# An attention layer's two key triangles folded into one block of 128, and GpSimd weight splits cut into pieces of 256 columns

## The chip, the cores and the metric

The kernel runs on one core of a Trainium2 chip. The metric is the device time of one execution in microseconds (us); of several runs the median is given. The engines are called as in the profile: PE (matmul) with PEld (its weight loads), DVE (vector), ACT (scalar), POOL (GpSimd) and SP, whose queue issues the DMA transfers.

## What is computed

A small decoder of two layers on an input of 2048 rows and 1024 columns in float32: first a gated retention layer, then a gated attention layer with a sliding window of 128 keys. The change lies in the second. Cut to what matters here:

```python
def band_bias_and_mask(rel_bias, nb):
    i = jnp.arange(BLOCK)[:, None]
    j = jnp.arange(2 * BLOCK)[None, :]
    dist = i + BLOCK - j
    ...
    in_window = (dist >= 0) & (dist < WINDOW)

def swa_layer(x, g_norm, w_in, g_q, sinks, w_out, k_band, v_band, bias, mask):
    proj = rmsnorm(x, g_norm) @ w_in
    q, gate = jnp.split(proj, [SWA_Q_WIDTH], axis=-1)
    q = rmsnorm(q.reshape(b, nb, BLOCK, SWA_KV_HEADS, SWA_GROUP, SWA_HEAD_DIM), g_q)
    scores = jnp.einsum('bnqkgd,bnjkd->bnkgqj', q, k_band).astype(jnp.float32)
    scores = scores * (SWA_HEAD_DIM ** -0.5) + bias[None, None]
    scores = jnp.where(mask[None, :, None, None], scores, -jnp.inf)
    m = jnp.maximum(jnp.max(scores, axis=-1, keepdims=True), sink)
    p = jnp.exp(scores - m)
    p = p / (jnp.sum(p, axis=-1, keepdims=True) + jnp.exp(sink - m))
    o = jnp.einsum('bnkgqj,bnjkd->bnqkgd', p.astype(v_band.dtype), v_band)
    o = o.reshape(b, s, SWA_Q_WIDTH) * jax.nn.silu(gate)
    return x + o @ w_out
```

BLOCK and WINDOW are both 128. A row block of 128 queries sees its own 128 keys and the 128 before. Query i may use key j of the block before when j > i, and key j of its own block when j <= i: for each j exactly one of the two. There are 16 query heads of 64 columns and 2 heads of keys and values, 8 query heads to each.

## The kernel before

Every projection is done in split precision. A weight tile of 128 partitions and 1024 columns (`wload`, L113) is loaded by SP, rounded by ACT into `whi` (L127), and the remainder is taken into `wlo` (L128 and L129): by DVE in the first layer and wherever a norm's scale has to be multiplied in first (L124), by POOL for all other weights of the second layer. `proj` (L132) then multiplies hi by hi, hi by lo and lo by hi: three matmuls where one would do in full precision, 24 of 512 columns to a tile.

The second layer is `phase_b` (L740). It works on four row groups of 512 rows (`g`) and, within each, on the two key heads (`kv`): eight units. Per unit there are these parts. `main` projects keys and values once per row group (`evac_kv`, L773: keys normalised, transposed and put into `kst`; values into `vst`) and then the queries (`evac_q`, transposed into `qst`, one half of them copied out of PSUM by DVE, L819, the other by ACT, L817). `gates` projects the gate. `attn` (L839) does the attention itself, `out_b` the output projection with the residual from memory; for the last unit `out_last` does it with the rows halved.

`attn` goes over four row blocks (`m`) and, in each, over two parities (`par`) with four heads `j` each; I call one parity of one row block a half block. Per half block: two matmuls per head give scores against up to 256 keys (L870). One DVE instruction (L873) adds the bias, negates, writes the result to `pt` and takes its least value over sink and row into `nm`. The bias is -1e30 where the window forbids a key. ACT takes the exponential with its row sum (L881). DVE adds the sink's term, takes the reciprocal and scales each head's row (L887). PE transposes each 128 by 128 piece (L891), four heads to a PSUM bank, one bank for each of the two key blocks `b`; ACT copies the first bank out (L897), DVE the second (L895). Once both parities are there, PE multiplies by the values (L907), block by block into one bank, and DVE and ACT apply the gate and split the result (L910 to L912). The very first row block has only its own keys, so `nb` is 1 there and 2 elsewhere.

Between row groups `stats` and `prep` (L183) make the next group's input: SP loads a tile, POOL multiplies it by the rows' norms (L189), ACT rounds it (L191) and DVE takes the remainder (L192), four times.

What order the work has: `drive` (L44) interleaves the parts by hand. `filler` (gates, the output projection of the unit before with the next group's prep in it, the next unit's `main`) and `attn` are generators, and `drive` takes them in turn by a ratio of 0.6, with `attn` issued at a higher priority (AHEAD). The order on each engine is then settled ahead of time by the framework's scheduler, from estimated durations; each engine works through its list in order. PSUM banks: two each for scores (`s`), for transposes and attention outputs (`f`), and four for projections.

## Time and profile before

| | us |
|---|---|
| median of 3 runs (2522.0 to 2522.67) | 2522.36 |
| the profiled execution | 2513.12 |
| its span, first to last instruction | 2511.3 |
| PE busy | 2446.6 |
| DVE busy | 1714.5 |
| ACT busy | 1128.1 |
| POOL busy | 477.2 |

The profiled execution is one run of its own, so its time differs a little from the median. Busy time of an engine is the union of its instructions; PE's includes modelled ends of pipelined matmuls. In a row of a group, "idle before" is the time in which the engine stood still just ahead of such an instruction, with what it waited for. In the chain of waits each piece is the work (or wait) that the end of the span depended on at that time. "Granted clock" is the share of full speed that PE was given: 1.00 is full.

### The profile page before, as it was taken

What the parts mean: (1) busy time and instruction counts of PE and PEld (TensorE: products, weight loads), DVE (VectorE), ACT (ScalarE), POOL (GpSimd) and SP (SyncE); (2) the same over time, 40 slices, a digit from 0 to 9 for tenths busy, and PEclk for the clock granted to TensorE, in tenths of its full rate; (3) what the DMA queues carried; (4) which work ended last, traced back from release to release, by engine and by line L of the source; (5) the groups of instructions that cost most, each with busy time, mean ns of one, the idle gap of its engine ahead of it and who ended that gap; (6) DMA issues with size and microseconds to landing.
All of it is one profiled execution on the core that took longest, in us unless ns stands there. A gap on an engine that the chain in (4) does not pass through costs nothing.

```text
span 2511.3 us, 32377 instructions
## 1 busy us (share of the span) xinstructions
PE 2446.6 (97%) x11816; PEld 1995.4 (79%) x11816; DVE 1714.5 (68%) x2953; ACT 1128.1 (45%) x2008; POOL 477.2 (19%) x393
## 2 busy tenths in 40 slices
PE   8999999999999999999999999989899999999998
PEld 6888787888888888888888888777677777777887
DVE  5546674786868657667666576677867677677766
ACT  4333233544436445435354354435544455445553
POOL 0000000021000020000010000042335444353360
PEclk9999999999999999999999999999899999999999
DMA  8434873586636455465364243374233342342432
GB/s 294 135 115 132 262 268 119 162 290 228 229 119 201 147 168 159 158 212 184 119 206 152 91 159 111 103 256 156 76 118 122 105 156 74 132 144 84 135 116 94
DMA packets 141035, 395.05 MB, mean 157 GB/s; under 512 B 16411, under 2 KB 28876, under 8 KB 140876
## 3 DMA queue, kind: packets, MB, share of 16 engines
q1 hardware_dynamic: 140876, 392.99, 47.3%
q8 instruction: 93, 1.52, 0.2%
q14 instruction: 66, 0.54, 0.1%
HBM read 321.60 MB, written 74.47 MB: 158 GB/s over the span
## 4 chain that ended last, share of the span: by engine, by line
PE 81%; DMA 8%; DVE 7%; ACT 2%; issue 1%; POOL 0%; SPq 0%; DVEq 0%; ACTq 0%
PE pp_ao L151 4%; PE pp_ao L149 4%; PE pp_ao L150 4%; PE o_t L907 2%; PE s_t L870 2%; PE pT_t L891 2%; PE pp_bo L149 1%; PE pp_bo L150 1%; PE pp_bo L151 1%; DMA res<-xmid 1%; PE ot_r L643 1%; PE dl_r L607 1%; PE o_r L615 1%; PE dl_r L608 1%; PE o_r L617 1%
## 5 line engine op out<-in xcount | busy, mean ns | idle before, releaser
L149 PE MATMUL pp_ao<-ohi_r,whi_ao 128*128 128x512 f32 x512 | 199.7, 394 | 4.9 <-DVE x_r L679 2.7
L150 PE MATMUL pp_ao<-olo_r,whi_ao 128*128 128x512 f32 x512 | 201.7, 394 | 0.0
L107 POOL TENSOR_SCALAR r_o_r<-sso_r,ep 128x1 f32<-128x1 f32 x48 | 28.6, 596 | 904.6 <-ACT jo_r L637 904.6
L881 ACT ACTIVATE P_t<-P_t,nm_t 128x256 f32<-128x256 f32 (+1 forms) x256 | 127.7, 499 | 157.3 <-DVE nm_t L873 156.7
L151 PE MATMUL pp_ao<-ohi_r,wlo_ao 128*128 128x512 f32 x512 | 196.7, 394 | 0.1
L873 DVE CUSTOM_DVE_ANT_0 P_t<-s_t,bias,nsnk 128x256 f32<-128x256 f32 (+1 forms) x256 | 116.5, 470 | 36.8 <-PE s_t L870 35.8
L127 ACT CAST whi_ao<-raw_ao 128x1024 fp32r<-128x1024 f32 x64 | 67.2, 1050 | 153.1 <-issue 47.5
L129 DVE TENSOR_TENSOR wlo_ao<-raw_ao,whi_ao 128x1024 fp32r<-128x1024 f32 x64 | 78.1, 1223 | 81.7 <-ACT whi_ao L127 80.3
L703 ACT CAST Shi_r<-S 128x512 fp32r<-128x512 f32 x120 | 69.9, 618 | 116.5 <-PE o_r L617 88.0
L149 PEld LDWEIGHTS pp_ao<-ohi_r,whi_ao 128*128 128x128 f32 x512 | 96.9, 189 | 26.0 <-DVE x_r L679 3.1
L151 PEld LDWEIGHTS pp_ao<-ohi_r,wlo_ao 128*128 128x128 f32 x512 | 97.1, 190 | 21.7 <-DVE wlo_ao L129 1.1
L150 PEld LDWEIGHTS pp_ao<-olo_r,whi_ao 128*128 128x128 f32 x512 | 97.4, 190 | 20.5 <-issue 0.2
L704 DVE TENSOR_TENSOR Slo_r<-S,Shi_r 128x512 fp32r<-128x512 f32 x120 | 85.4, 737 | 40.1 <-ACT Shi_r L703 39.9
L870 PE MATMUL s_t<-kst,qst_b 128*128 128x256 f32 (+1 forms) x512 | 103.3, 299 | 8.6 <-DVE nm_t L873 8.5
L870 PEld LDWEIGHTS s_t<-kst,qst_b 128*128 128x128 f32 x512 | 84.8, 193 | 30.8 <-DVE nm_t L873 11.5
L630 DVE SCALAR_TENSOR_TENSOR S<-S,dl_r 128x512 f32<-128x512 f32 x112 | 74.6, 682 | 41.4 <-PE dl_r L609 41.3
L887 DVE TENSOR_SCALAR P_t<-P_t,den_t 128x256 f32<-128x256 f32 (+1 forms) x256 | 95.0, 434 | 1.8
L679 DVE TENSOR_TENSOR x_r<-x_r,pp_ao 128x512 f32<-128x512 f32 x128 | 84.0, 683 | 14.1 <-PE pp_ao L151 14.0
L149 PE MATMUL pp_bo<-ohi_t,whi_bo 128*128 128x512 f32 x224 | 89.1, 406 | 1.3 <-DVE gate_b L834 1.1
L150 PE MATMUL pp_bo<-olo_t,whi_bo 128*128 128x512 f32 x224 | 89.0, 397 | 0.0
L129 POOL TENSOR_TENSOR wlo_bo<-raw_bo,whi_bo 128x1024 fp32r<-128x1024 f32 x28 | 70.5, 2523 | 93.9 <-ACT whi_bo L127 80.0
L151 PE MATMUL pp_bo<-ohi_t,wlo_bo 128*128 128x512 f32 x224 | 87.7, 396 | 0.0
(1037 smaller groups left out, 7464.1 us busy)
## 6 DMA issues: line engine op xcount, KB each, us to landing
raw_ao<-in_wo_a SPq DMA_DIRECT2D x64, 512.0 KB, 3.6
b<-in_w_vg SPq DMA_DIRECT2D x64, 256.0 KB, 5.1
res<-xmid SPq DMA_DIRECT2D x56, 256.0 KB, 3.0
raw_bo<-in_wo_b SPq DMA_DIRECT2D x28, 512.0 KB, 3.6
x_r<-in_x_t SPq DMA_DIRECT2D x16, 512.0 KB, 5.8
xin<-in_x SPq DMA_DIRECT2D x16, 512.0 KB, 3.5
xmid<-x_r SPq DMA_DIRECT2D x16, 512.0 KB, 4.3
xraw_b<-xmid SPq DMA_DIRECT2D x16, 512.0 KB, 3.6
```

Of the source, the lines that this page charges most:

```text
L129: eng.tensor_tensor(lo, raw, hi.bitcast(F32), op=ALU.subtract)
L149: nc.tensor.matmul(o, hi[:, kk, sl], xh, start=st, stop=False)
L150: nc.tensor.matmul(o, hi[:, kk, sl], xl, start=False, stop=False)
L151: nc.tensor.matmul(o, lo[:, kk, sl], xh, start=False, stop=sp)
L630: nc.vector.scalar_tensor_tensor(S32[:, d, :], S32[:, d, :], gamC[h], dl[d], op0=ALU.mult, op1=ALU.add)
L679: nc.vector.tensor_tensor(t, t, ps, op=ALU.add)
L703: nc.scalar.copy(hi, src[:, d, :])
L704: nc.vector.tensor_tensor(lo, src[:, d, :], hi.bitcast(F32), op=ALU.subtract)
L870: nc.tensor.matmul(o, qst[m][:, h, :], kst[:, kv * 2 + hl, kb + b0 : kb + 2, :], start=hl == 0, stop=hl == 1)
L873: nc.vector.tensor_tensor_reduce(out=pt[:, j, :w], in0=o, in1=bias[:, kv * GQ + h, b0 * P :], scale=-1.0, scalar=nsv[:, h : h + 1], op0=AL ...
L881: nc.scalar.activation(pt[:, j, :w], pt[:, j, :w], AF.Exp, scale=-1.0, bias=nm[:, c : c + 1], accum_out=den[:, c : c + 1])
L887: nc.vector.tensor_scalar_mul(pt[:, j, :w], pt[:, j, :w], den[:, c : c + 1])
```

## The change

In the attention, each pair of heads' 256 columns is folded: after the scores of two heads are reduced, DVE takes the minimum of the left and right 128 columns (the forbidden one of each pair is +1e30 after the negation). The exponential, its sum, the scaling (now one instruction for four heads) and the transposes work on 128 columns. Of the transposed bank ACT writes one copy as it is, and DVE a second one multiplied by a triangular mask, loaded once. The values are held twice: as they are, and as differences from the block before. The plain copy is multiplied by the values of the block before, the masked copy by the differences; their sum is the former result. The four exponentials of a half block are issued after all four score rows instead of each after its own.

Beside it: POOL takes a weight tile's remainder in four pieces of 256 columns instead of one instruction; the multiplication in `prep` goes from POOL to DVE; and two kinds of copies out of PSUM (the first half of the transposed queries, the transposed keys) go from DVE to ACT.

```diff
+PIECE = 256
...
-        eng = nc.gpsimd if psum["phase"] == "b" and kscale is None else nc.vector
-        eng.tensor_tensor(lo, raw, hi.bitcast(F32), op=ALU.subtract)
+        if psum["phase"] == "b" and kscale is None:
+
+            for k in range(kn):
+                for c in range(0, cols, PIECE):
+                    t = (slice(None), k, slice(c, c + PIECE))
+                    nc.gpsimd.tensor_tensor(lo[t], raw[t], hi[t].bitcast(F32), op=ALU.subtract)
+        else:
+            nc.vector.tensor_tensor(lo, raw, hi.bitcast(F32), op=ALU.subtract)
...
-            nc.gpsimd.tensor_tensor(raw, raw, rb.unsqueeze(1).to_broadcast([P, 2, T]), op=ALU.mult)
+            nc.vector.tensor_tensor(raw, raw, rb.unsqueeze(1).to_broadcast([P, 2, T]), op=ALU.mult)
...
+        mask = cst.tile([P, P], F32, name="mask_b")
+        nc.sync.dma_start(mask, mask_t)
...
-                vst = p2.tile([P, MT, KVH * HD], F32, tag="vst", name=f"vst_{n}")
+
+                vst = p2.tile([P, 2, MT, KVH * HD], F32, tag="vst", name=f"vst_{n}")
...
-                    nc.vector.tensor_copy(vst[:, m, :], kr[:, KVH * HD : 2 * KVH * HD])
+                    v = vst[:, 0, m, :]
+                    nc.vector.tensor_copy(v, kr[:, KVH * HD : 2 * KVH * HD])
+                    if g or m:
+                        before = (vst if m else st["kv", g - 1])[:, 0, (m - 1) % MT, :]
+                        nc.vector.tensor_tensor(vst[:, 1, m, :], v, before, op=ALU.subtract)
...
-                    nc.vector.tensor_copy(kst[:, :, kb + m + 1, :], tp.rearrange("p (a t) -> p a t", a=4))
+                    nc.scalar.copy(kst[:, :, kb + m + 1, :], tp.rearrange("p (a t) -> p a t", a=4))
...
-                    if half:
-                        nc.scalar.copy(dst, t3)
-                    else:
-                        nc.vector.tensor_copy(dst, t3)
+                    nc.scalar.copy(dst, t3)
...
+                        if j % 2 and nb == 2:
+
+                            pj = pt[:, j - 1 : j + 1, :]
+                            nc.vector.tensor_tensor(pj[:, :, :P], pj[:, :, :P], pj[:, :, P:], op=ALU.min)
                         if j == 3:
                             sn = snv.rearrange("p (j t) -> p t j", t=2)[:, par, :]
                             nc.vector.tensor_tensor(es[:, hs], sn, nm[:, hs], op=ALU.add)
                             nc.scalar.activation(es[:, hs], es[:, hs], AF.Exp)
-                        nc.scalar.activation(pt[:, j, :w], pt[:, j, :w], AF.Exp, scale=-1.0,
+                    for j in range(4):
+                        c = 4 * par + j
+                        nc.scalar.activation(pt[:, j, :P], pt[:, j, :P], AF.Exp, scale=-1.0,
                                              bias=nm[:, c : c + 1], accum_out=den[:, c : c + 1])
                     nc.vector.tensor_tensor(den[:, hs], den[:, hs], es[:, hs], op=ALU.add)
                     nc.vector.reciprocal(den[:, hs], den[:, hs])
+                    pw = pt[:, :, :P]
+                    nc.vector.tensor_tensor(pw, pw, den[:, hs].unsqueeze(2).to_broadcast([P, 4, P]), op=ALU.mult)
+                    tp = bank(f"pT_{n}_{m}_{par}", "f")
                     for j in range(4):
-                        c = 4 * par + j
-                        nc.vector.tensor_scalar_mul(pt[:, j, :w], pt[:, j, :w], den[:, c : c + 1])
+                        nc.tensor.transpose(tp[:, j * P : (j + 1) * P], pt[:, j, :P], ident)
+                    t = [p2.tile([P, 512], F32, tag=f"pT{par}", name=f"pTs_{n}_{m}_{b}_{par}") for b in range(nb)]
+                    nc.scalar.copy(t[0], tp)
+                    if nb == 2:
+
+                        a4 = lambda x: x.rearrange("p (a t) -> p a t", a=4)
+                        nc.vector.tensor_tensor(a4(t[1]), a4(tp), mask.unsqueeze(1).to_broadcast([P, 4, P]),
+                                                op=ALU.mult)
                     for b in range(nb):
-                        tp = bank(f"pT_{n}_{m}_{b}_{par}", "f")
-                        for j in range(4):
-                            nc.tensor.transpose(tp[:, j * P : (j + 1) * P],
-                                                pt[:, j, b * P : (b + 1) * P], ident)
...
-                    vv = (cur if blk >= 0 else prev)[:, blk % MT, kv * HD : (kv + 1) * HD]
+                    vv = (cur if blk >= 0 else prev)[:, 1 if b else 0, blk % MT, kv * HD : (kv + 1) * HD]
...
-                    nc.gpsimd.tensor_tensor(lo, raw, hi.bitcast(F32), op=ALU.subtract)
+                    for k in range(2):
+                        for c in range(0, T, PIECE):
+                            t = (slice(None), k, slice(c, c + PIECE))
+                            nc.gpsimd.tensor_tensor(lo[t], raw[t], hi[t].bitcast(F32), op=ALU.subtract)
```

More of the change, by code (lines that the diff above doesn't have):

```diff
@@ L138, in proj @@
             hi, lo = wload(src[kp], cols, f"{name}_{kp}",
-                           None if kscale is None else kscale[:, kp * kn : (kp + 1) * kn], (key, kp))
+                           None if kscale is None else kscale[:, kp * kn : (kp + 1) * kn],
+                           (key, kp))
             for kk in range(kn):
@@ L884, in attn @@
                     nc.vector.reciprocal(den[:, hs], den[:, hs])
+                    pw = pt[:, :, :P]
+                    nc.vector.tensor_tensor(pw, pw, den[:, hs].unsqueeze(2).to_broadcast([P, 4, P]), op=ALU.mult)
+                    tp = bank(f"pT_{n}_{m}_{par}", "f")
                     for j in range(4):
-                        c = 4 * par + j
-                        nc.vector.tensor_scalar_mul(pt[:, j, :w], pt[:, j, :w], den[:, c : c + 1])
-                    for b in range(nb):
-                        tp = bank(f"pT_{n}_{m}_{b}_{par}", "f")
-                        for j in range(4):
-                            nc.tensor.transpose(tp[:, j * P : (j + 1) * P],
-                                                pt[:, j, b * P : (b + 1) * P], ident)
-                        t = p2.tile([P, 512], F32, tag=f"pT{par}", name=f"pTs_{n}_{m}_{b}_{par}")
-                        if b:
-                            nc.vector.tensor_copy(t, tp)
-                        else:
-                            nc.scalar.copy(t, tp)
-                        pT[b, par] = t
+                        nc.tensor.transpose(tp[:, j * P : (j + 1) * P], pt[:, j, :P], ident)
[5 more added lines that the diff above has]
+                                                op=ALU.mult)
+                    for b in range(nb):
+                        pT[b, par] = t[b]
                     yield
```

## The prediction, made before the result

> **What bounds the kernel now.** I read the page's busy shares first, then the busy time by stretches of the second layer, then the chain of waits, then single groups. Busy shares:
>
> ```profile
> span 2511.3 us, 32377 instructions
> PE 2446.6 (97%) x11816; PEld 1995.4 (79%) x11816; DVE 1714.5 (68%) x2953; ACT 1128.1 (45%) x2008; POOL 477.2 (19%) x393
> ```
>
> The whole kernel is a queue of matmuls with everything else beside it. The change touches only the second layer, from about 1640 us on (and the hand-over into it), so I cut that into stretches; the columns are length, then busy time of PE, PEld, DVE, ACT and POOL, then the granted clock.
>
> ```profile
> core 0: us, PE busy (x) PEld busy (x) DVE busy (x) ACT busy (x) POOL busy (x), PEclk, DMA share, GB/s
> 1640.00:1726.00 86.00, 77.40 (x403) 65.69 (x402) 63.37 (x117) 37.92 (x67) 31.68 (x27) 0.94 0.68 239
> 1726.00:1781.00 55.00, 55.00 (x286) 44.16 (x286) 47.35 (x115) 30.47 (x74) 19.49 (x15) 1.00 0.36 122
> 1781.00:1804.00 23.00, 14.75 (x57) 9.25 (x55) 20.98 (x47) 11.59 (x29) 7.60 (x3) 0.63 0.35 115
> 1804.00:2010.00 206.00, 204.08 (x1070) 158.13 (x1070) 141.44 (x361) 97.27 (x240) 85.85 (x53) 1.00 0.32 106
> 2010.00:2030.00 20.00, 18.04 (x89) 14.64 (x88) 18.71 (x34) 13.20 (x28) 11.88 (x6) 0.91 0.45 152
> 2030.00:2215.00 185.00, 180.64 (x969) 142.44 (x968) 126.50 (x330) 91.48 (x224) 81.09 (x51) 1.00 0.32 108
> 2215.00:2265.00 50.00, 44.26 (x240) 35.08 (x239) 37.02 (x76) 23.91 (x55) 24.00 (x10) 1.00 0.55 186
> 2265.00:2456.00 191.00, 188.97 (x1021) 152.55 (x1019) 136.75 (x343) 102.21 (x245) 85.57 (x51) 1.00 0.34 112
> 2456.00:2512.00 56.00, 45.77 (x317) 37.64 (x315) 33.38 (x112) 16.43 (x53) 0.00 (x0) 0.95 0.25 85
> sum 872.00, PE 828.92 PEld 659.57 DVE 625.50 ACT 424.48 POOL 347.15; mean PE 92.10 PEld 73.29 DVE 69.50 ACT 47.16 POOL 38.57
> ```
>
> The three long stretches (582 us) have PE busy for 573.7 us, 98.6%: there the number of matmuls sets the time. The short stretches at 1781, 2010 and 2215 are where the next row group's input is prepared; DVE is nearly full there and PE stands still 8.3, 2.0 and 5.7 us, with the clock down to 0.63 in the first. DVE (72% of 872 us), ACT (49%) and POOL (40%) have room elsewhere.
>
> **The change part by part.** *Transposes.* The chain of waits gives what one projection matmul and what eight transposes hold of the path (start, length, engine, output, line, count):
>
> ```profile
> 2448.30 0.23 PE pp_bo L149
> ...
> 2451.85 0.87 PE pT_t L891 x8
> ```
>
> Group L891 (its row stands below) has 496 transposes. A full block has two key blocks times two head parities times four heads; folded, half of that: 60 banks of four go and 256 transposes stay. Four take half of 0.87, 0.435 us, and 60 x 0.435 = 26.1 us of PE. The product with the values stays at two matmuls per parity and block (plain values by all weights, differences by the masked ones), the scores stay, so nothing returns to PE. Where PE is 98.6% busy this is path. The four stretches where PE stands still (1781, 2010, 2215 and the tail from 2456) are 149 of the 872 us, 17%; a saving there may be lost in other waits. So 21.7 to 26.1, and I take 26.1.
>
> *DVE, ACT and POOL work.* First the groups that go, move or serve as prices (count | busy us, mean ns | idle before), then the least, median and greatest ns of one instruction of a line, last one exponential of 128 columns:
>
> ```profile
> L891 PE MATMUL pT_t<-ident_r,P_t 128*128 128x128 f32 x496 | 78.2, 281 | 1.0 <-ACT qst_b L817 0.4 <-ACT pTs_t L897 0.3 <-DVE P_t L887 0.2
> L887 DVE TENSOR_SCALAR P_t<-P_t,den_t 128x256 f32<-128x256 f32 x240 | 91.4, 444 | 1.7
> L895 DVE COPY pTs_t<-pT_t 128x512 f32<-128x512 f32 x60 | 41.3, 688 | 31.0 <-PE pT_t L891 31.0
> ...
> L819 DVE CAST qst_b<-qtp_b 128x512 fp32r<-128x512 f32 x32 | 21.9, 683 | 1.3 <-PE qtp_b L813 1.3
> L817 ACT CAST qst_b<-qtp_b 128x512 fp32r<-128x512 f32 x32 | 18.6, 582 | 5.5 <-PE qtp_b L813 5.4
> L189 POOL TENSOR_TENSOR xraw_b<-xraw_b,rb 128x1024 f32<-128x1024 f32 x16 | 43.0, 2692 | 32.1 <-DVE ssq_b L799 12.6 <-DMA xraw_b<-xmid 10.6 <-DVE rb L180 7.6
> ```
>
> ```profile
> L962 DVE TENSOR_TENSOR res_l<-res_l,pp_l x16: 412/422/423, 2476.8 to 2507.7; 128x256 f32<-128x256 f32 x16
> L805 DVE TENSOR_TENSOR qs_b<-qn_b,qs_b x32: 679/692/2868, 1702.7 to 2430.2; 128x512 fp32r<-128x512 f32 x32
> L192 DVE TENSOR_TENSOR xlo_b<-xraw_b,xhi_b x16: 1210/2109/3024, 1640.0 to 2234.3; 128x1024 fp32r<-128x1024 f32 x16
> L881 ACT ACTIVATE P_t<-P_t,nm_t x256: 387/509/544, 1713.1 to 2486.3; 128x256 f32<-128x256 f32 x120, 128x128 f32<-128x128 f32 x8
> L129 POOL TENSOR_TENSOR wlo_bo<-raw_bo,whi_bo x28: 2377/2406/3384, 1773.0 to 2444.6; 128x1024 fp32r<-128x1024 f32 x28
> L691 POOL TENSOR_TENSOR acc<-acc,sqx x28: 1259/1616/2138, 502.0 to 1662.0; 128x512 f32<-128x512 f32 x28
> ```
>
> ```profile
> 1804.13 0.40 ACT L881 ACTIVATE P_t<-P_t,nm_t 128x128 f32<-128x128 f32 x1 [3.48 <-DVE nm_t L873]
> ```
>
> DVE loses the scalings by 1/den (91.4 us), the second copy of a transposed bank (41.3) and the casts that go to ACT (32 at 21.9, and 16 of the keys at the same 0.68, 10.9): 165.5. It gets 120 minima of 2 x 128 columns at 0.42 (nearest row L962; as much as a 512-column row, 0.69, if the strided halves cost double), 50; 64 broadcast multiplications of 512 columns at 0.69 (L805), 44; 60 masked copies at 0.69, 41; 15 value differences at 0.42 at most (128 columns), 6; and the 16 multiplications of prep that POOL did, at the 1.21 of L192, 19. Sum 160 to 193: about even. ACT: 240 exponentials fall from 0.51 to 0.40 us, -26, and 48 casts come at 0.58, +28: even. POOL: 512 columns cost 1.26 and 1024 cost 2.38 at least, so 0.14 us an instruction and 0.56 per 256 columns; a piece takes 0.70 and a weight tile 2.8 instead of 2.4. With 86 tiles (28 and 4 of the output projections, 18 for each of three row groups) that is +34, against -43.0 for the prep work. All three have room beside PE in the long stretches, so I cost these totals at nothing; that cover is thin only in the first two prep stretches, where DVE is 91 and 94% busy; where it is gone, each us of DVE work is a us of PE.
>
> *The prep stretches.* The chain through the worst one, then POOL's own rows, then the same four scalings when POOL is quiet:
>
> ```profile
> 1776.04 2.29 DVE den_t L883
> 1778.56 5.44 DVE P_t L887 x4
> ...
> 1785.41 2.62 DVE xlo_b L192
> 1794.32 2.62 DVE xlo_b L192
> ```
>
> ```profile
> 1778.54 2.41 POOL L129 TENSOR_TENSOR wlo_bo<-raw_bo,whi_bo 128x1024 fp32r<-128x1024 f32 x1 [0.24 <-ACT whi_bo L127]
> 1780.90 2.42 POOL L189 TENSOR_TENSOR xraw_b<-xraw_b,rb 128x1024 f32<-128x1024 f32 x1
> ```
>
> ```profile
> 2470.85 1.06 DVE P_t L887 x4
> ```
>
> Four scalings take 5.44 us instead of 1.06 while two POOL instructions run back to back until 1783.3, and end 0.7 us after the second: DVE stands until POOL's instruction is over. The longest L192 lies 1.8 us over its least, the longest L805 2.2. In this stretch the holds on the chain are 4.4 (scalings), 1.9 or more (the sum L883 has four columns, and 256 need 0.42) and 2 x 1.4 (xlo): some 9 us. In pieces a hold is at most 0.70, and the second holder, L189, leaves POOL, for 4 x 1.21 us of DVE per prep. What PE loses in the stretch is 8.3 us of standing and (1 - 0.63) x 23 = 8.5 us of clock, 16.8; at 2010 it is 2.0 + 1.8; at 2215 5.7, of which most of the chain is the residual's round trip through memory, which stays. I take half of the first two and 1 us of the third: -11. Bounds: nothing, if the DVE work added fills what the holds free, and -22.
>
> The Trainium skill (SBUF — State Buffer, section Who interferes with whom) says that GpSimd and a DVE instruction that uses the second port or has two SBUF inputs exclude each other for a whole instruction, whichever came first. The 5.44 us agree. It also speaks against the change: the minima, the broadcast multiplication and the moved prep work have two SBUF inputs, so DVE may now hold POOL between pieces (third rival). The skill's TensorE: Matmul & The Clock Gate, section Part 1, says that an idle window of about 3.4 us halves the clock; if the standing goes, by that rule the 8.5 us go with it, which would make the sum some 4 us lower than mine.
>
> *The attention chain.* The scores' reduction stays, but a minimum follows each pair, and the four exponentials are issued after the second one. From the last score read to the first transpose, apart from a sum and a reciprocal that stay: before, the last exponential 0.51 and the scalings 1.06, 1.6 us; after, the minimum 0.42, four exponentials 4 x 0.40 and one multiplication 0.69, 2.7 us. That is 1.1 us longer per half block (one parity of one 128-row block, 64 in all). On DVE the third score read is queued behind the first minimum, and PE's next scores wait for that read to free their bank. PE's longest entry in the table of waits (us in total, times, longest):
>
> ```profile
> PE s_t L870 <- DVE nm_t L873: 8.5, 7, 3.2
> ```
>
> Seven waits for a score bank, and for P itself 0.2 us in all (end of the L891 row): the chain runs ahead of PE. I charge 0.42 for each of the seven, +3 (0 to +10, if 64 half blocks paid 0.16 each). The casts moved to ACT free their bank 0.6 us later per half, before scores that are a unit away: nothing, unless ACT is in a burst; it is 49% busy. The mask's load is one more transfer on SP's queue ahead of the first weights of the layer; its nearest row is
>
> ```profile
> 1670.09 0.48 SPq L738 DMA_DIRECT2D gk<-in_kng  x1
> ```
>
> so +0.5, in a stretch where PE waits for loads. Its prep multiplications pass from POOL to a DVE that is 74% busy there: 0, between -3 and +3.
>
> *Sum:* -26.1 - 11 + 3 + 0.5 = -33.6 us, against the profiled execution's 2513.1 us (span 2511.3). The median of the runs is 2522.4, 9.2 us above it; taking the difference over gives 2489 us.
>
> **The rivals.** *The prep stalls go entirely* (holds gone, clock up): -26 - 22 + 3 = -45, 2477. For it: the stall chain is made of holds. Against: 4.9 us of DVE work come into each of the three prep stretches. Chance 0.17.
>
> *The gain is swallowed.* The order of instructions is laid out anew from estimated durations; a few new waits of 2 to 4 us each at unit borders eat part of it: -21.7 + 10 + 3.5 = -8, 2514. For it: PE stands at such borders now, 4.4 us in the stretch from 2030. Chance 0.17, a quarter of it within 0.2% (5 us, about what a measurement of this kernel can tell from no change).
>
> *POOL falls behind.* If DVE takes the port after each piece for 0.69 us, a tile needs 4 x 1.39 = 5.6 us. PE takes 872 / 86 = 10.1 us per tile with the attention between, and POOL's other work (347 - 43 - 86 x 2.4 = 98 us) 1.1 of them. So from 9.0 us a tile on, tiles come late; at 0.5 us late each, 86 x 0.5 - 26 = +17, 2539, slower. For it: bursts of projection alone need a tile every 24 x 0.23 = 5.5 us. Against: even a 1.21 us hold after every piece gives 7.6. Chance 0.04.
>
> *The chain becomes the bound,* slower too: exposed fully, 64 x 1.1 = 70 - 26 = +44, 2566; it cancels the saving from 0.41 us per half block on. For it: it has two steps more. Against: PE hardly waits for P now, and a half block has 872 / 64 = 13.6 us of PE to hide 2.7 us in. Chance 0.03.
>
> **How the numbers follow.** Forecast 2489 with its own cases (2480 to 2500), 0.59. To 2470 for the full end of the stalls and of the saving, to 2512 for half of the swallowed case: that leaves out some 0.04 below and 0.15 above. Faster by over 0.2%: 0.59 + 0.17 + three quarters of 0.17 = 0.89; same 0.04; slower 0.07.
>
> **What would show it.** 256 transposes in group L891's place and 26 us less PE busy in the second layer; POOL pieces near 0.70 us; longest holds on DVE under 1 us; a granted clock of 1.00 around 1781 to 1804; PE's waits for score banks under 12 us. Wrong would be PE busy falling by 26 while the span does not: then the waits table names what came instead; or weight tiles from POOL among those that PE waits for.

## The result, and the profile after

The changed kernel takes 2534.39 us (median of 5 runs, 2531.89 to 2543.54), the kernel before 2522.36 (2519.37 to 2524.05). The ratio is 1.0054, 95% interval 1.0034 to 1.0074: slower by 12 us, where 33 us less were forecast. The profiled execution after took 2535.16 us. Its page begins:

```profile
span 2533.3 us, 32135 instructions
PE 2458.3 (97%) x11576; PEld 1977.5 (78%) x11576; DVE 1668.3 (66%) x2864; ACT 1126.1 (44%) x2056; POOL 501.4 (20%) x635
```

240 matmuls are gone, and PE is busy 11.7 us longer. The busy time by stretches shows the second layer, then the three stretches where PE now stands still (length, busy time of PE, PEld, DVE, ACT, POOL, granted clock):

```profile
1640.00:2534.00 894.00, 844.95 (x4223) 646.26 (x4221) 583.68 (x1443) 424.88 (x1058) 375.62 (x455) 0.97 0.37 124
```

```profile
1785.00:1808.00 23.00, 15.56 (x79) 10.77 (x78) 21.13 (x59) 16.45 (x49) 6.42 (x7) 0.85 0.39 134
2090.00:2110.00 20.00, 12.97 (x45) 6.72 (x44) 8.99 (x22) 9.18 (x23) 3.61 (x6) 0.76 0.09 27
2224.00:2240.00 16.00, 11.59 (x50) 8.58 (x47) 14.45 (x20) 9.66 (x16) 8.65 (x8) 0.79 0.31 102
```

The first stretch is the old prep stall: the clock falls less deep (0.85 for 0.63), but PE stands 7.4 us there, where it stood 8.3. The second is new: no engine is full there, so it is a chain that holds PE, not a load. The groups of the change, in the second layer (count | busy us, mean ns | idle before):

```profile
L925 PE MATMUL o_t<-pTs_t,vst_b 128*64 128x512 f32 x248 | 98.9, 633 | 6.9 <-DVE pTs_t L913 4.8 <-ACT pTs_t L909 2.0
L134 POOL TENSOR_TENSOR wlo_bo<-raw_bo,whi_bo 128x256 fp32r<-128x256 f32 x112 | 93.3, 866 | 87.7 <-ACT whi_bo L128 87.7
L892 DVE TENSOR_TENSOR P_t<-P_t 128x256 f32<-128x256 f32 x120 | 65.6, 558 | 1.3
L904 DVE TENSOR_TENSOR P_t<-P_t,den_t 128x512 f32<-128x512 f32 x64 | 46.7, 730 | 1.5
L907 PE MATMUL pT_t<-ident_r,P_t 128*128 128x128 f32 x256 | 45.0, 289 | 9.9 <-DVE P_t L904 9.6 <-ACT pTs_t L909 0.3
L913 DVE TENSOR_TENSOR pTs_t<-pT_t,mask_b 128x512 f32<-128x512 f32 x60 | 41.1, 685 | 27.1 <-ACT pTs_t L909 27.0
```

The transposes have 256 instructions and 33.2 us less busy time than the 78.2 before. But the products with the values (L925) have as many records, of the same shape, and take 98.9 us. Before, their row was:

```profile
L907 PE MATMUL o_t<-pTs_t,vst_b 128*64 128x512 f32 x248 | 68.4, 618 | 2.2 <-ACT pTs_t L897 2.2
```

The mean of one record hardly moved (618 to 633 ns); the busy time, which counts overlapping records once, rose by 30.5. So what changed is how far they overlap. PE's timeline shows it. One product (one head parity, one key block) is two records. Before, the four products of a row block:

```profile
1857.66 1.94 PE L907 MATMUL o_t<-pTs_t,vst_b 128*64 128x512 f32 x8
```

After, the four products of a row block:

```profile
1767.43 1.07 PE L925 MATMUL o_t<-pTs_t,vst_b 128*64 128x512 f32 x2
1768.43 0.50 PE L157 MATMUL pp_b1g<-xhi_b,whi_b1g 128*128 128x512 f32 x1
...
1772.64 1.08 PE L925 MATMUL o_t<-pTs_t,vst_b 128*64 128x512 f32 x4
1773.65 0.62 PE L882 MATMUL s_t<-kst,qst_b 128*128 128x256 f32 x3
1774.20 1.07 PE L925 MATMUL o_t<-pTs_t,vst_b 128*64 128x512 f32 x2
```

The weights are 64 columns wide (128\*64); the first parity writes partitions 0 to 63 of the output's bank, the second 64 to 127. Two products of different parity (x4) take 1.08 us, and one alone (x2) takes 1.07: in a pair the second starts 7 ns after the first and costs nothing. Before, four products filled two slots of about 1 us. Now the first one is issued alone, then a pair, then the last one alone: three slots. Counted in the trace, the products stand before in 25 unbroken runs of 8 records, 5 of 6, 1 of 4 and 7 of 2; after in 2 of 8, 9 of 6, 20 of 4 and 49 of 2. Two products to a slot where they can pair, that is 68 slots before and 91 after. From the first record of each run to the next other matmul, they hold PE 67.3 us before and 99.6 after.

To see where all the time went, I cut the second layer, from its first matmul (1654.2 us before, 1661.0 after) to the end, by the time from each matmul's start to the next one's; idle time then falls to the matmul that it follows. The layer starts 6.8 us later after the change; over all kernels here that start lies between 1652.6 and 1661.0, and at 1660.2 in the kernel before with only its products in another order, so I don't put it down to the change. "Half clock" is the time at which the granted clock is 0.5. "Lost" is PE's idle time and half of the time at half clock; "in prep" is the part of it in the three stretches in which the next row group is prepared, each from the first gate projection of a row group's second unit to the next group's first key projection. "Held" is the sum, over DVE's instructions, of the time beyond the shortest of the same line and shape. All in us, from one profiled execution of each kernel:

| kernel | layer 2 | PE idle | half clock | lost | in prep | products | transposes of P | scores | transposes of q, k | projections | held |
|---|---|---|---|---|---|---|---|---|---|---|---|
| before | 857.2 | 38.5 | 34.5 | 55.8 | 22.5 | 67.3 | 54.5 | 74.7 | 34.4 | 622.4 | 124 |
| after | 872.3 | 44.3 | 47.0 | 67.7 | 23.4 | 99.6 | 32.4 | 88.4 | 41.4 | 606.3 | 72 |
| pieces and moves | 846.0 | 28.8 | 33.7 | 45.6 | 19.2 | 67.6 | 53.3 | 78.8 | 31.9 | 610.4 | 67 |
| pieces alone | 848.8 | 32.6 | 29.9 | 47.6 | 14.0 | 69.4 | 54.7 | 77.1 | 33.3 | 610.6 | 71 |
| after, paired | 837.4 | 42.5 | 42.1 | 63.6 | 22.9 | 63.7 | 29.3 | 86.9 | 40.3 | 612.9 | 64 |
| fold alone | 887.5 | 55.2 | 58.0 | 84.2 | 29.1 | 99.2 | 33.5 | 99.0 | 33.4 | 618.5 | 133 |
| fold alone, paired | 865.4 | 60.4 | 73.5 | 97.2 | 37.4 | 67.5 | 28.6 | 102.4 | 34.9 | 628.2 | 139 |

Before to after: transposes -22.1, projections -16.1, products +32.3, scores +13.7, transposes of queries and keys +7.0; sum +14.8 of the +15.1. The first term is the gain that was forecast for the transposes. The second is for the most part standing that has changed its place: PE stands 12.5 us less behind projections and 18.3 us more behind the other matmuls, and what it loses in the prep stretches is as before (22.5 and 23.4). The third is not in the prediction at all; without the standing and the loss at half clock behind the products it is +26.0 (64.0 to 90.0).

### The profile page after: what moved, and what is told of

It is laid out like the page before. It is cut to its first block, busy times and chain, and to the rows that moved or that the text cites. A ratio compares the mean times of both kernels' runs of the same rounds, so it can differ in the third digit from the quotient of the medians.

```text
span 2533.3 us, 32135 instructions
## 1 busy us (share of the span) xinstructions
PE 2458.3 (97%) x11576; PEld 1977.5 (78%) x11576; DVE 1668.3 (66%) x2864; ACT 1126.1 (44%) x2056; POOL 501.4 (20%) x635
## 4 chain that ended last, share of the span: by engine, by line
PE 80%; DMA 8%; DVE 7%; ACT 2%; issue 1%; POOL 1%; SPq 0%; DVEq 0%; ACTq 0%; POOLq 0%
PE pp_ao L159 4%; PE pp_ao L157 4%; PE pp_ao L158 4%; PE o_t L925 3%; PE s_t L882 2%; PE pp_bo L158 2%; PE pp_bo L159 2%; PE pp_bo L157 2%; DMA b<-in_w_vg 1%; PE pT_t L907 1%; PE ot_r L651 1%; PE dl_r L615 1%; PE dl_r L616 1%; PE o_r L623 1%; PE o_r L625 1%
## 5 line engine op out<-in xcount | busy, mean ns | idle before, releaser
L899 ACT ACTIVATE P_t<-P_t,nm_t 128x128 f32<-128x128 f32 x256 | 100.8, 394 | 118.0 <-DVE P_t L892 113.3
L134 POOL TENSOR_TENSOR wlo_bo<-raw_bo,whi_bo 128x256 fp32r<-128x256 f32 x112 | 93.3, 866 | 87.7 <-ACT whi_bo L128 87.7
L925 PE MATMUL o_t<-pTs_t,vst_b 128*64 128x512 f32 x248 | 98.9, 633 | 6.9 <-DVE pTs_t L913 4.8
L638 DVE SCALAR_TENSOR_TENSOR S<-S,dl_r 128x512 f32<-128x512 f32 x112 | 74.5, 681 | 41.4 <-PE dl_r L617 41.3
```

Source lines behind the costliest of these rows:

```text
L134: nc.gpsimd.tensor_tensor(lo[t], raw[t], hi[t].bitcast(F32), op=ALU.subtract)
L638: nc.vector.scalar_tensor_tensor(S32[:, d, :], S32[:, d, :], gamC[h], dl[d], op0=ALU.mult, op1=ALU.add)
L899: nc.scalar.activation(pt[:, j, :P], pt[:, j, :P], AF.Exp, scale=-1.0, bias=nm[:, c : c + 1], accum_out=den[:, c : c + 1])
L925: nc.tensor.matmul(op[par * HD : (par + 1) * HD, :], vv, pT[b, par], start=b == 0, stop=b == nb - 1)
```

## The experiments

**Theory A**: the products lost their partners, and these slots took the gain back. The rivals: the loss comes from the longer attention chain, from the PSUM banks, or from the other parts of the change.

**Pairs restored.** The changed kernel, with one dependency more.

```diff
-                    nc.scalar.copy(t[0], tp)
+                    cp = [nc.scalar.copy(t[0], tp)]
...
-                        nc.tensor.matmul(op[par * HD : (par + 1) * HD, :], vv, pT[b, par],
-                                         start=b == 0, stop=b == nb - 1)
+                        mm = nc.tensor.matmul(op[par * HD : (par + 1) * HD, :], vv, pT[b, par],
+                                              start=b == 0, stop=b == nb - 1)
+                        if par == 0:
+                            tc.add_manual_dep(mm.ins, cp[b].ins.name, mybir.DependencyInfo(
+                                mybir.DependencyClass.Sync, mybir.DependencyReason.DATA), reason="pair")
```

Here `cp` holds the second parity's copies when the products are written, so the first parity's product waits for its partner's data.

> The changed kernel, with one thing added: the first parity's product of a key block waits for the second parity's copy of the same block, so that the two products of a block stand next to each other in PE's order (62 slots of one or two products instead of 91; before the change 68). Theory A, lost pairs: two neighbouring products that fill different halves of the array run at once (1.01 us for the two, as for one alone), so 29 slots fewer are 29 us less: about 2505 us, 0.7% under the kernel before, and the group of products falls from 98.9 us busy to about 63. Rival B, the longer attention chain: the time went into waits for P and its copies; pairing makes products wait longer, so 2530 to 2545. Rival C, POOL's pieces or the moved work: pairing does not touch them, so no more than 5 us less than the changed kernel's 2534.

Measured: 2500.67 us, ratio to the kernel before 0.9929 (0.9912 to 0.9945). Against the changed kernel's 1.0054 that is 1.25%, some 31 us, for one added wait. PE's timeline has the four products of the same row block in two pairs, and the group's busy time is 66.0 us:

```profile
1772.13 1.08 PE L925 MATMUL o_t<-pTs_t,vst_b 128*64 128x512 f32 x4
1773.14 0.50 PE L882 MATMUL s_t<-kst,qst_b 128*128 128x256 f32 x2
1773.48 0.40 PE L159 MATMUL pp_b1g<-xhi_b,wlo_b1g 128*128 128x512 f32 x1
1773.81 1.08 PE L925 MATMUL o_t<-pTs_t,vst_b 128*64 128x512 f32 x4
```

```profile
L925 PE MATMUL o_t<-pTs_t,vst_b 128*64 128x512 f32 x248 | 66.0, 624 | 3.3 <-ACT pTs_t L909 2.7 <-DVE pTs_t L913 0.6
```

By the table the products give back 35.9 us (99.6 to 63.7), the whole layer 34.9 (872.3 to 837.4). Theory A stands, and this version beats both kernels.

**The kernel before, its products in another order.** The two loops around the products exchanged:

```diff
-                for b in range(nb):
-                    blk = m - 1 + b0 + b
-                    vv = (cur if blk >= 0 else prev)[:, blk % MT, kv * HD : (kv + 1) * HD]
-                    for par in range(2):
+                for par in range(2):
+                    for b in range(nb):
+                        blk = m - 1 + b0 + b
+                        vv = (cur if blk >= 0 else prev)[:, blk % MT, kv * HD : (kv + 1) * HD]
```

> The kernel before, with the two loops around the products exchanged (parity outside, key block inside), which leaves every instruction and only changes PE's order: 93 slots instead of 68. Theory A: 25 slots more at 1.0 us, so about 2547 us, 1.0% slower than before, and the group of products near 93 us busy. Rivals B and C: nothing but the order of four neighbouring products changes, so within 3 us of before.

Measured: 2524.82 us, ratio 1.0019 (1.0009 to 1.0029), 4.6 us and not 25: a miss. The trace shows why, and it sharpens the theory. The four products still stand next to each other, and although the program's order is now parity 0, 0, 1, 1, they take the same 1.94 us:

```profile
1769.35 1.94 PE L907 MATMUL o_t<-pTs_t,vst_b 128*64 128x512 f32 x8
```

Their records start in pairs 13 ns apart, where it was 7; which product a record belongs to the trace does not say. So this order inside an unbroken run does not matter; in these traces a product is alone only when matmuls of another kind stand between it and its partner. The products held PE 67.6 us, as before.

**One PSUM bank.** The changed kernel, where the output's bank now can't be had before the second parity's transposes are copied:

```diff
-PSUM_BUFS = {"rr": 4, "s": 2, "f": 2}
+PSUM_BUFS = {"rr": 4, "s": 2, "f": 1}
```

> The changed kernel, with one PSUM bank instead of two for transposes and attention outputs. It tests why the order changed. Theory A says: in the changed kernel a half block needs one transposed bank instead of two, so the output's bank is free before the second parity is transposed and the first product is issued alone; with one bank it can't be. The order built from it has 62 slots, as in the run with the pairs kept: about 2505 us if the missing bank costs nothing, up to 2525 if transposes have to wait for copies. Rival B (the chain from scores to products sets the time): one bank lengthens that chain, so slower than the changed kernel, 2540 or more.

Measured: 2566.99 us, ratio 1.0188 (1.0172 to 1.0203). All products stand in pairs in the program's order, which agrees with the reading of the code that the freed bank is what lets the first product go early: before, four transposed banks pass through the two banks ahead of the output's, in the changed kernel two. But a single bank makes PE wait for each copy:

```profile
PE o_t L925 <- DVE pTs_t L913: 21.5, 10, 3.8
PE pT_t L907 <- DVE pTs_t L913: 16.3, 9, 4.4
```

PE's idle time in the layer goes to 83.9 us. As a cure it is worse than the loss.

**Without the fold.** The kernel before with the pieces on POOL, the prep multiplication on DVE and the copies on ACT, by the lines of the change's own diff:

```diff
+                    nc.gpsimd.tensor_tensor(lo[t], raw[t], hi[t].bitcast(F32), op=ALU.subtract)
...
+            nc.vector.tensor_tensor(raw, raw, rb.unsqueeze(1).to_broadcast([P, 2, T]), op=ALU.mult)
...
+                    nc.scalar.copy(kst[:, :, kb + m + 1, :], tp.rearrange("p (a t) -> p a t", a=4))
...
+                    nc.scalar.copy(dst, t3)
```

> The kernel before, with all of the change but the fold: POOL in pieces of 256 columns, prep's multiplication on DVE, the two kinds of casts on ACT. 70 slots of products, against 68 before. Theory A: no pairs are lost, so what is left is shorter holds of DVE against 36 us more of POOL: between 2510 and 2525, the prediction's own estimate being 11 us less than before. Rival C: these parts make the change slow, so 2532 or more.

Measured: 2510.9 us, ratio 0.9957 (0.9942 to 0.9973): 9 us faster. So the rest of the change is worth 9 to 11 us without the fold, and the fold as written costs what is left, 24 us. Only 3.3 us of the gain lie in the prep stretches (22.5 to 19.2).

**The fold alone**: the changed kernel without the pieces and the moves.

```diff
-                    nc.gpsimd.tensor_tensor(lo[t], raw[t], hi[t].bitcast(F32), op=ALU.subtract)
+        eng.tensor_tensor(lo, raw, hi.bitcast(F32), op=ALU.subtract)
...
-            nc.vector.tensor_tensor(raw, raw, rb.unsqueeze(1).to_broadcast([P, 2, T]), op=ALU.mult)
+            nc.gpsimd.tensor_tensor(raw, raw, rb.unsqueeze(1).to_broadcast([P, 2, T]), op=ALU.mult)
...
-                    nc.scalar.copy(dst, t3)
+                    if half:
+                        nc.scalar.copy(dst, t3)
+                    else:
+                        nc.vector.tensor_copy(dst, t3)
```

> The kernel before with the fold alone: GpSimd's subtractions whole, the multiplication of the residual stream on GpSimd, and the copies of transposed queries and keys on VectorE as before. The order that the scheduler writes for TensorE has 34 pairs of products with the values and 56 single ones, 90 slots, where the kernel before has 68. Theory A (a product that is cut off from its partner of the other parity takes about 1.0 us of its own, and in the changed kernel these slots take back what the 240 missing transposes give): the fold alone costs what the changed kernel costs over the run without the fold (ratios 1.0054 and 0.9957), 24 us, so about 2545, and in any case not under 2525. Theory B (the fold gains its 26 us, and the moved copies and pieces lose it): 2500 or less.

Measured: 2547.86 us, ratio 1.0115 (1.0101 to 1.013), 30 us slower than before. Theory A's 2545 holds; theory B, that the fold gains and the rest loses, is refuted.

**The fold alone, pairs restored**: both edits together.

> The fold alone, with the product of the first parity made to wait for the copy of the second parity, so that TensorE's order has 62 pairs and no single product. Theory A: 28 slots of 1.0 us less than the fold alone with single products, so 25 to 35 us faster than that kernel; against the kernel before it is worth what the paired run gained over the run without the fold (0.9929 against 0.9957), 7 us, so about 2513. If pairing only helps where ScalarE and VectorE carry the moved work, the two kernels with the fold alone lie within 8 us of each other.

Measured: 2524.8 us, ratio 1.0028 (1.0016 to 1.0041). The pairs give 22 us, a little less than the 25 to 35 expected, but the kernel is 7 us slower than before, not 7 faster. The parts don't add up: PE idles 60.4 us, against 42.5 with the whole change. Its waits, and DVE's minima:

```profile
PE pT_t L904 <- DVE P_t L901: 13.5, 6, 5.6
PE s_t L879 <- DVE nm_t L882: 12.7, 11, 2.9
```

```profile
L889 DVE TENSOR_TENSOR P_t<-P_t 128x256 f32<-128x256 f32 x120 | 82.7, 695 | 1.2
```

A minimum takes 0.70 us in the mean, with a median of 0.42 and a greatest of 2.62: DVE is held 139 us in all where the paired whole change has 64. With the paired fold the rest of the change is worth about 25 us (1.0028 to 0.9929), without it 9 to 11; the last runs ask which part.

**Exponentials earlier.** The paired kernel, with the exponentials of two heads right after the minimum of these two:

```diff
-                    for j in range(4):
-                        c = 4 * par + j
+                        if j % 2:
+                            for i in (j - 1, j):
+                                c = 4 * par + i
...
```

> The changed kernel with paired products, and the exponentials of two heads issued right after the minimum of these two heads, in place of after all four. In the paired run TensorE is busy 17.6 us less than in the run without the fold between 1640 us and the end, but idle 14 us more. Chain theory (this idle time is the half block's longer chain from scores to transposes, of which the late exponentials are one piece of about 1 us on each half block): 3 to 10 us faster than the paired run's 2500.7, so 2491 to 2498. Rival (ScalarE takes the exponentials in the same places anyway, because the scheduler fills it with other work, and the idle time comes from VectorE's two added steps, which stay): within 3 us of the paired run, 2498 to 2504.

Measured: 2503.13 us, ratio 0.9942 (0.993 to 0.9954), where the paired kernel has 0.9929 (0.9912 to 0.9945): no gain. The late exponentials are not what makes the chain long.

**Both parities in one half.** The kernel before, with an edit that lets all products write the first 64 partitions and leaves out the other half of the output:

```diff
-                        nc.tensor.matmul(op[par * HD : (par + 1) * HD, :], vv, pT[b, par],
-                                         start=b == 0, stop=b == nb - 1)
+                        nc.tensor.matmul(op[:HD, :], vv, pT[b, par],
+                                         start=b + par == 0, stop=b + par == nb)
...
-                nc.vector.tensor_tensor(og, og, op.rearrange("p (a t) -> p a t", a=4), op=ALU.mult)
+                nc.vector.tensor_tensor(og[:HD], og[:HD], op[:HD].rearrange("p (a t) -> p a t", a=4), op=ALU.mult)
```

> The kernel before, but all products with the values of a row block write and sum into the first 64 partitions of the output's bank, so that none lies beside a product of the other parity; the second 64 partitions of the gate are not multiplied, so the output is not the attention's. Number of instructions and their shapes are as before, neighbours in the order stay neighbours. Theory A (two neighbouring products take the time of one because they fill different column halves of the array): 124 slots of about 0.95 us where there were 68, so 50 to 58 us more busy time of TensorE, and 45 to 58 us slower than before, 2565 to 2580. Rival (neighbours overlap because nothing stands between them, whichever half they fill, as the exchanged loops might suggest, which cost only 4.6 us): the products take 67 us as before, and the kernel is within 6 us of the kernel before.

Measured: 2572.12 us, ratio 1.0208 (1.0191 to 1.0225): 54 us slower. The same eight records, side by side as before, take 3.65 us instead of 1.94:

```profile
1766.96 3.65 PE L907 MATMUL o_t<-pTs_t,vst_b 128*64 128x512 f32 x8
```

```profile
L907 PE MATMUL o_t<-pTs_t,vst_b 128*64 128x512 f32 x248 | 120.2, 623 | 2.1 <-ACT pTs_t L897 2.1
```

The mean record is again 623 ns and tells nothing; the union, 120.2 us, does. The products hold PE 119.0 us instead of 67.3, and these 51.7 us come out as 54 us of time: a slot of a product is on the path at its full price.

**Which part the fold needs.** Four runs: the kernel before with POOL's pieces alone (the first hunk of the diff of "Without the fold"); and the paired kernel less one part at a time, by the hunks of the diff of "The fold alone": with whole POOL tiles (the first), with the prep multiplication back on POOL (the second), and with the copies of queries and keys back on DVE (the third, and the same for `kst`).

> The kernel before with GpSimd's subtractions in pieces of 256 columns, and nothing else. The run without the fold gained 9.4 us with the pieces and the moved work together, and VectorE's time over the shortest duration of each of its instructions, which is where GpSimd holds it, fell from 130 to 69 us there. If the pieces did this (VectorE is held for at most one piece of 0.74 us, not for 2.4): 4 to 10 us faster than before, with VectorE's time over the minimum at 60 to 85 us. If the moved work did it (65 us less busy time of VectorE), the pieces alone are within 3 us of the kernel before.

> The changed kernel with paired products, but GpSimd's subtractions whole, 2.4 us each. Theory: the fold's new steps on VectorE have two inputs and are held by a long GpSimd instruction (in the run of the fold alone with paired products VectorE spent 144 us over the shortest durations, in the paired run of the whole change 67), and their ends stand in the chain from scores to transposes, so TensorE waits: 6 to 20 us slower than the paired run's 2500.7, 2507 to 2520. Rival (the moved copies made the difference between these two runs): within 4 us of the paired run.

> The changed kernel with paired products and pieces, but the multiplication of the residual stream (2.4 us each, whole) stays on GpSimd. VectorE has about 16 instructions of 1.2 us less, and is held by the long instruction in the stretches where the next group is prepared. If these holds are what stalls the stretches at 1790, 2010 and 2215 us, as the prediction had it: 3 to 8 us slower than the paired run, 2504 to 2509. If VectorE's load decides: 0 to 6 us faster, 2495 to 2501.

> The changed kernel with paired products and pieces, but the copies of the transposed keys and of half of the transposed queries stay on VectorE: about 48 copies of 0.6 to 0.7 us, some 30 us more busy time there and as much less on ScalarE. If VectorE's load makes the waits of the fold alone (60 us idle on TensorE where the paired run has 42): 8 to 18 us slower than the paired run, 2509 to 2519. If the long GpSimd instructions make them: within 4 us of the paired run's 2500.7.

Measured ratios to the kernel before: pieces alone 0.9953 (0.9941 to 0.9964); paired with whole tiles 0.9970 (0.9958 to 0.9982); paired with the prep multiplication on POOL 0.9997 (0.9985 to 1.001); paired with the copies on DVE 0.9953 (0.9941 to 0.9965). Without the fold the pieces give all that pieces and moves give together (0.9957): 11 us, a little over the 4 to 10 expected. With the fold, against the paired 0.9929, whole tiles cost 10 us, as expected; the copies on DVE 6, between the two expectations, though the two intervals overlap; and 16 multiplications on POOL 17, far over the 3 to 8 expected. The whole tiles cost where DVE is held: PE loses 40.7 us in the prep stretches, for 22.9. So the pieces are worth about as much with the fold (10) as without it (11).

The multiplications on POOL hold DVE too. POOL's row in that kernel, then DVE's and PE's, in the first prep:

```profile
1781.43 5.58 POOL L197 TENSOR_TENSOR xraw_b<-xraw_b,rb 128x1024 f32<-128x1024 f32 x2
```

```profile
1782.35 2.44 DVE L904 TENSOR_TENSOR P_t<-P_t,den_t 128x512 f32<-128x512 f32 x1
```

```profile
1787.04 0.51 PE L882 MATMUL s_t<-kst,qst_b 128*128 128x256 f32 x2 [4.06 <-DVE nm_t L885]
```

The multiplication of P, 0.69 us otherwise, takes 2.44. Behind it in DVE's list stand three steps of the gate (1.87 us) and then the reduction of scores for which PE waits 4.06 us. The Trainium skill (SBUF — State Buffer, section Who interferes with whom) says that a DVE instruction with two SBUF inputs and a GpSimd one that reads SBUF exclude each other; by that rule each of the fold's two new kinds of step can be held. This trace agrees, with 2.44 for 0.69 us.

But these holds are not what most of the 17 us is made of. PE loses no more in the prep stretches of that kernel than in the paired one (22.5 and 22.9 us), and outside them 65.3 instead of 40.7, where POOL has no such multiplication to do. The longest of these waits stand at the ends of units; first this kernel's, then the paired kernel's at the same place:

```profile
2086.40 1.09 PE L907 MATMUL pT_t<-ident_r,P_t 128*128 128x128 f32 x4 [4.79 <-DVE P_t L904]
2083.50 0.63 PE L907 MATMUL pT_t<-ident_r,P_t 128*128 128x128 f32 x4 [1.97 <-DVE P_t L904]
```

In the paired kernel seven projection matmuls follow the last scores and cover the chain; in the other there are none. So most of the 17 us lies outside the stretches where these multiplications run, and a part of it in how late the new order puts a unit's last half block; why it does so was not followed.

## Why the prediction was wrong

*Transposes, -26.1.* The count (256) and the size were right: from start to start they take 54.5 us before, 32.4 after and 29.3 paired, so -22 to -25. The step that failed stands in the same paragraph: "The product with the values stays at two matmuls per parity and block ..., so nothing returns to PE." The count stayed, the time did not. A matmul's price depended on its neighbour: pairing puts two products into one slot of 1.0 us, and with the fold the first product went before its partner's data were there (as the code reads, because fewer banks are needed ahead of the output's). That is +32.3 us, of which 26.0 are slots alone. That the lost pairs are the cause is shown by restoring them, and the price of a slot by the run in one half. The row that should have warned was in the trace of before: 248 records of 618 ns are 153 us, and the group is busy 68.4. Whoever prices by groups should ask of such a row with which neighbour it overlaps, and whether the change keeps that neighbour. The Trainium skill (TensorE: Matmul & The Clock Gate, section Part 3: Packing small matmuls) says that matmuls whose outputs lie in different column groups run at the same time, about 4 ns apart; the traces agree that they overlap, and have 7 ns.

*DVE, ACT and POOL totals, at nothing.* Right in the totals: DVE's busy time fell (625.5 to 583.7 us from 1640 us on) because its holds fell (124 to 72), ACT's stayed (424.5, 424.9). POOL's pieces are 0.72 us at least, as estimated (0.70), but 0.87 in the mean in the output projections. That is hardly the fold's doing, since without it the pieces take 0.84 and 0.85 there. PE's waits name no weight tile of POOL's, so the third rival did not happen.

*Prep stretches, -11.* The second step that failed: in the changed kernel this gain did not come. PE loses 22.5 us there before, 23.4 after and 22.9 paired. The pieces alone bring it to 14.0, so they free about what was forecast (8.5), and the idea of the holds is borne out: a minimum takes at most 1.00 us (median 0.42), where scalings and sums stood 2.2 us over their least before. With the moved work it is 19.2, and with the fold's steps nothing is left; that is the lower bound that I had named, "if the DVE work added fills what the holds free". Which of the added steps fill it is not shown. The 9 us of the run without the fold come near the -11 by luck, since only 3.3 of them lie here. The clock in the first stretch is 0.85, not the 1.00 that I named.

*The attention chain, +3 (0 to +10).* Mis-sized. Outside the prep stretches PE loses 33.3 us before, 40.7 in the paired kernel (+7.4) and 44.3 after (+11.0, over the upper bound). Against the run without the fold it is more: from there to the paired run, transposes and products give 27.9 us less, the layer only 8.6. Of the 19.3 us between, 13.7 are idle time of PE and 4.2 the price of 8.4 us more at half clock. Scores and the transposes of queries and keys, the instructions after which PE now stands, hold 16.5 us more. I charged seven waits for a score bank; the new cost is in good part a few long waits at the ends of units, where no projection is left to cover the chain. The chain of waits of the changed kernel shows the longest:

```profile
2091.67 0.25 PE s_t L882 x2
2091.93 0.03 issue
2091.95 0.48 DVE P_t L885
2092.44 0.01 DVE nm_t L885
2092.45 0.40 DVE P_t L885
2092.84 0.01 DVE nm_t L885
2092.85 0.69 DVE P_t L892
2093.54 0.60 DVE pTs_t L913
2094.14 0.33 DVE P_t L892
2094.47 0.61 DVE es_t L895
...
2095.32 0.39 ACT P_t L899 x2
...
2096.14 0.70 DVE P_t L904
2096.84 0.14 issue
2096.97 0.36 PE pT_t L907
```

From the last score (2091.9) to the first transpose (2097.0) PE stands 5 us: two minima of P (L892), a masked copy of the other parity that DVE takes between them (0.60) and the multiplication (0.70) lie in it. The first of the minima and the sum before the exponential (`es_t`, 0.68 here, 0.15 in the paired kernel) stand beside POOL's pieces, which run from 2092.53 to 2095.74, and last longer than elsewhere. The exponentials, which the prediction counted as most of the lengthening, take 0.39 there, and issuing them earlier changed nothing. PE's waits of the changed kernel name the same (us, times, longest):

```profile
PE pT_t L907 <- DVE P_t L904: 9.6, 6, 4.8
PE s_t L882 <- DVE nm_t L885: 6.0, 8, 1.6
PE o_t L925 <- DVE pTs_t L913: 4.8, 2, 4.7
```

The score-bank waits stayed under the 12 us that I set; I had looked for the chain in the wrong row. In the paired kernel the first of these is 4.6 us.

*The mask's load, +0.5.* No wait for it appears among PE's waits, and it can't be told from the scatter of the layer's start.

*The rivals.* "The gain is swallowed" is nearest: the order laid out anew did eat it. But it was priced at new waits of a few us at unit borders, 2514; those came, and the lost pairs, 32 us, are no wait at all. With the pairs the kernel gives 2501, inside the range, but by other terms than forecast: the transposes are there, the prep's gain is not, and the chain costs more than +3. "Wrong would be PE busy falling by 26 while the span does not" was not what came: PE's busy time rose.

What stays open: why the scheduler's order costs the prep multiplications on POOL 17 us and the copies on DVE 6 was not followed further, and that the freed bank is the reason for the early product is read from the code and agrees with the run with one bank; no run changed the bank alone without new waits.

## What to carry to other kernels

Before counting instructions as unchanged, compare a group's busy time with its count times its mean: where busy is much less, the instructions share time with a neighbour, and a change that separates them costs a full slot each. A resource that comes free earlier (here, as the code reads, a PSUM bank) can make an order worse; when data of two partners are needed together, say so with a dependency. And a total that comes out near the forecast says little about its terms: the run without the fold gained about the forecast 11 us, but only a third of it in the stretches it was forecast for.

## What the runs showed of the hardware

Two products of 64 columns each in different halves of the array take 1.01 us from start to next start, one alone 1.00; two in the same half about 1.9. Pairing does not need partners next to each other in the program's order: parities 0, 0, 1, 1 in an unbroken run still take 1.94 us for four, with pairs starting 13 ns apart; matmuls that fill the whole width between them break it. After the 5 us wait at 2092 us the granted clock is at half for 6.8 us from 2097 us on (mean of the stretch 0.76), and the row of the two products there is 1.90 us long instead of 1.0: a wait in the chain costs more than its own length.
